# A rule that holds back side steps: when DeltaNet and attention matmuls enter the stream of weight matmuls in a hybrid decoder layer

## The chip, the cores and the metric

The kernel runs on one core of one Trainium2 chip. The metric is the device time of one execution in microseconds (us), the median of several runs. The core's engines work side by side, each through its own instructions in order: TensorE (PE: matmuls and transposes), VectorE (DVE), ScalarE (ACT), GpSimd (POOL) and SyncE (SP, which issues the DMAs). An instruction that waits for an operand holds up everything behind it on its engine.

## The reference

One decoder layer for 256 positions of width 1024 in fp32: a pre-norm, a joint input projection, two parallel branches, a gated merge, an output projection and a SwiGLU feed-forward block.

```
h = rms_norm(x, norm_mix_pre)
proj = h @ w_in                       # 1024 -> 9232: qa ka va qd kd vd zd bd ad ga gd
ya = moba_attention(rope(qa), rope(ka), va)      # 8 heads of 128, here one causal block of 256
yd = gated_deltanet(qd, kd, vd, zd, bd, ad, ...) # conv, silu, l2 norm, chunks of 64, 8 heads
merged = sigmoid(ga) * (ya @ w_o_attn) + sigmoid(gd) * (yd @ w_o_delta)
x = x + rms_norm(merged @ w_out, norm_mix_post)
h = rms_norm(x, norm_ffn_pre)
x = x + rms_norm((silu(h @ w_gate) * (h @ w_up)) @ w_down, norm_ffn_post)
# in the DeltaNet, per head and chunk: A = I + strict(beta k k^T * decay); T = A^-1 (unit lower triangular);
# u, w = T v_beta, T k_beta; then the state runs over the chunks; o = rms_norm(o) * silu(z)
```

## The kernel before

**Weight stream.** Most of PE's time goes into the weight matmuls, called main here. A weight matrix is cut into pieces of 128 x 1024 (824 or 828 in the gate columns). A piece is loaded into `wr` (4 buffers), ACT rounds it to `wh` (the high half), DVE subtracts to get `wl` (the low half), and three matmuls (high x high, high x low, low x high) make an fp32-accurate product. `wh` and `wl` have 5 buffers each, so that the `wh` of piece j waits until PE has done with piece j-5. `split_to` issues both operations three pieces ahead of their use. Main runs through the list `UNITS`: `c` (DeltaNet q, k, v by channel), `a` (attention q, k, v), `z`, `g` (gates), then `oa` and `od` (the branches' output projections), `wo`, and the feed-forward block. `oa` starts only when both attention generators are done, `od` when both of the DeltaNet's outputs are.

**Side steps.** The small matmuls of the branches (transposes through `tr`, L294; products through `mm`, L290) are made by generators: `dn` (a DeltaNet tile: group g of four heads, half t of the positions), `dno` (the DeltaNet's recurrence and output, per group), `at` (attention of four heads at a time) and `gates`. A DeltaNet tile computes k normalised (`d_kn`), its transpose `d_kh`, the matrix `h_a`, and inverts it in six levels with `h_U`, `h_T` and the level matrices `wl2` to `wl64` (traced as `wl`, 128x64 matmuls in fp16, four per step). At its end `dno` forms the output `d_oA`: ACT squares and sums four heads into `tiny` through `scr`, DVE, POOL (a power) and DVE again make a scale, four DVE operations SCALAR_TENSOR_TENSOR multiply by scale and `d_sz` (the silu of z), and PE transposes `d_oA` into `q_ydh` and `q_ydl`. A generator stops at `yield At(tiles)` until a built-in estimate of the engines' clocks says that the tiles are there (plus `MARGIN`, 50 ns), or for so many ns.

**What sets the order.** Class `Flow` keeps the estimated PE time `t`. Every main matmul group yields, and `run` then calls `pump`, which lets every generator whose time has come do its step, oldest first. Whatever a step issues on PE is put behind the main matmul that was last. The order on all engines is thus fixed when the program is built, by estimates; on the chip nothing is rearranged. In the trace a main matmul writes a bank `b_m`, a side matmul a bank `b_s`. A visit is a run of side matmuls between two main ones. Every operation of ACT, DVE, POOL and SP has the line L132, of the wrapper that accounts for it.

Of the kernel before, what the change touches and what calls it, by code (L numbers as in the profile page):

```python
# [26 lines left out]
NFR = DFF // 512  # L27
PSUM = bass.MemoryType.PSUM
MARGIN = 50
STAG = 0  # L30
WARM = 5
DEC = 6
# [105 lines left out]
class Flow:  # L138
# [65 lines left out]
    def step(self, s):  # L204
# [10 lines left out]
        if isinstance(w, At):  # L215
            del s[4:]
            s[0] = max(self.rdy.get(n, 0.0) for n in w.names) + MARGIN
        elif callable(w):
# [6 lines left out]
    def ready(self, s):  # L225
        return s[0] <= self.t and (len(s) == 4 or s[4]())

    def pump(self):
        for s in sorted(self.side, key=lambda a: a[1]):
            if self.ready(s):  # L230
                self.step(s)
# [21 lines left out]
def build(nc, tc, ctx, A):  # L253
# [756 lines left out]
    def unit_c(u):  # L1010
# [13 lines left out]
        if dns[g] == 6:  # L1024
            fl.add(("dn", g, 0), dn_tile(g, 0))
            fl.add(("dn", g, 1), later(STAG, dn_tile(g, 1)))
            fl.add(("dno", g), after(("dn", g, 0), dn_out, g))
# [327 lines left out]
    def later(ns, gen):  # L1355
        yield ns
        yield from gen

    def after(name, f, *args):
        while name not in fl.done:  # L1360
            yield 500
        yield from f(*args)
# [27 lines left out]
```

## Time and profile before

| | before |
|---|---|
| median of 3 runs | 549.88 us (549.68 to 550.12) |
| profiled execution | 549.29 us, span 547.6 us |
| PE busy | 534.8 us (98%) |
| DVE busy | 368.1 us (67%) |
| ACT busy | 315.0 us (58%) |
| POOL busy | 26.4 us (5%) |

The span runs from the first to the last profiled instruction; the remaining 1.69 us of the profiled execution lie around it. Busy shares say how full an engine is, not whether somebody waits for it: a DVE that is 67% busy can still be late for one matmul.

### The profile page before, as it was taken

What the parts mean: (1) busy time and instruction counts of PE and PEld (TensorE: products, weight loads), DVE (VectorE), ACT (ScalarE), POOL (GpSimd) and SP (SyncE); (2) the same over time, 40 slices, a digit from 0 to 9 for tenths busy, and PEclk for the clock granted to TensorE, in tenths of its full rate; (3) what the DMA queues carried; (4) which work ended last, traced back from release to release, by engine and by line L of the source; (5) the groups of instructions that cost most, each with busy time, mean ns of one, the idle gap of its engine ahead of it and who ended that gap; (6) DMA issues with size and microseconds to landing.
All of it is one profiled execution on the core that took longest, in us unless ns stands there. A gap on an engine that the chain in (4) does not pass through costs nothing.

```text
span 547.6 us, 8378 instructions
## 1 busy us (share of the span) xinstructions
PE 534.8 (98%) x3156; PEld 460.6 (84%) x3156; DVE 368.1 (67%) x650; ACT 315.0 (58%) x553; POOL 26.4 (5%) x38
## 2 busy tenths in 40 slices
PE   7999999899999999999999999999999999999995
PEld 5988898898989888899889988778888888888884
DVE  4899876895879787866577567586465554554434
ACT  6868658487654965786526544585444544443331
POOL 0000002200000230000000000010000000000000
PEclk8999999999999999999999999999999999999998
DMA  8947765245455252244465766257666665555612
GB/s 258 255 149 216 218 197 150 78 117 167 129 168 158 78 167 64 63 148 155 131 201 187 247 210 195 77 158 259 202 189 193 180 197 176 181 189 192 193 38 78
DMA packets 63035, 90.40 MB, mean 165 GB/s; under 512 B 3233, under 2 KB 35090, under 8 KB 62994
## 3 DMA queue, kind: packets, MB, share of 16 engines
q1 hardware_dynamic: 62994, 89.86, 53.4%
q8 instruction: 25, 0.41, 0.3%
q14 instruction: 16, 0.13, 0.1%
HBM read 88.80 MB, written 1.05 MB: 164 GB/s over the span
## 4 chain that ended last, share of the span: by engine, by line
PE 85%; DVE 4%; ACT 3%; DMA 3%; issue 2%; POOL 2%; SPq 0%; POOLq 0%; DVEq 0%; ACTq 0%
PE b_m L290 73%; PE b_s L290 8%; PE b_s L294 2%; PE b_m L294 2%; DMA q_x<-in_x 1%; DVE wl L132 1%; POOL tiny L132 1%; DMA K<-in_shape_k 1%; DMA wr<-in_w_in 1%; ACT wh L132 1%; ACT L132 0%; DVE h_a L132 0%; DVE q_vT L132 0%; SPq L132 0%; ACT d_js L132 0%
## 5 line engine op out<-in xcount | busy, mean ns | idle before, releaser
L132 DVE TENSOR_TENSOR wl<-wr,wh 128x1024 fp32r<-128x1024 f32 (+3 forms) x168 | 197.8, 1184 | 120.8 <-ACT wh L132 116.9
L132 ACT ACTIVATE wh<-wr 128x1024 fp32r<-128x1024 f32 (+3 forms) x168 | 171.8, 1030 | 151.6 <-PE b_m L290 142.9
L290 PE MATMUL b_m<-wh,q_fh 128*128 128x512 f32 x264 | 103.5, 392 | 0.5 <-DVE q_fl L132 0.5
L290 PE MATMUL b_m<-wl,q_fh 128*128 128x512 f32 x264 | 103.0, 390 | 0.0
L290 PE MATMUL b_m<-wh,q_fl 128*128 128x512 f32 x264 | 102.7, 390 | 0.0
L290 PE MATMUL b_m<-wh,q_hh 128*128 128x512 f32 (+2 forms) x208 | 83.1, 400 | 1.0 <-ACT wh L132 1.0
L290 PE MATMUL b_m<-wl,q_hh 128*128 128x512 f32 (+2 forms) x208 | 78.8, 379 | 0.0
L290 PE MATMUL b_m<-wh,q_hl 128*128 128x512 f32 (+2 forms) x208 | 78.8, 379 | 0.0
L290 PEld LDWEIGHTS b_m<-wh,q_fh 128*128 128x128 f32 x264 | 49.6, 188 | 11.0 <-DVE q_fl L132 1.0
L290 PEld LDWEIGHTS b_m<-wl,q_fh 128*128 128x128 f32 x264 | 49.6, 188 | 10.7 <-DVE wl L132 0.7
L290 PEld LDWEIGHTS b_m<-wh,q_fl 128*128 128x128 f32 x264 | 49.5, 188 | 10.3
L290 PE MATMUL b_m<-q_hh,wh 128*128 128x256 f32 x192 | 56.3, 293 | 0.0
L290 PE MATMUL b_m<-q_hl,wh 128*128 128x256 f32 x192 | 54.4, 283 | 0.0
L290 PE MATMUL b_m<-q_hh,wl 128*128 128x256 f32 x192 | 54.4, 283 | 0.0
L290 PEld LDWEIGHTS b_m<-wh,q_hh 128*128 128x128 f32 x208 | 39.5, 190 | 5.4 <-ACT wh L132 1.5
L290 PEld LDWEIGHTS b_m<-wh,q_hl 128*128 128x128 f32 x208 | 39.5, 190 | 5.3
L290 PEld LDWEIGHTS b_m<-wl,q_hh 128*128 128x128 f32 x208 | 39.6, 190 | 4.3 <-DVE wl L132 0.5
L132 POOL TENSOR_TENSOR tiny<-tiny,mhalf 128x4 f32<-128x4 f32 (+1 forms) x20 | 17.4, 873 | 471.3 <-DVE tiny L132 471.3
L290 PEld LDWEIGHTS b_m<-q_hh,wh 128*128 128x128 f32 x192 | 36.7, 191 | 0.4
L290 PEld LDWEIGHTS b_m<-q_hl,wh 128*128 128x128 f32 x192 | 36.7, 191 | 0.3
L290 PEld LDWEIGHTS b_m<-q_hh,wl 128*128 128x128 f32 x192 | 36.7, 191 | 0.1
L132 ACT ACTIVATE h_U<-b_s 128x256 f16<-128x256 f32 (+1 forms) x28 | 11.5, 415 | 10.9 <-PE b_s L290 10.9
(204 smaller groups left out, 718.0 us busy)
## 6 DMA issues: line engine op xcount, KB each, us to landing
wr<-in_w_in SPq DMA_DIRECT2D x56, 512.0 KB, 3.8
wr<-in_w_down SPq DMA_DIRECT2D x22, 512.0 KB, 3.3
wr<-in_w_gate SPq DMA_DIRECT2D x20, 512.0 KB, 3.7
wr<-in_w_up SPq DMA_DIRECT2D x20, 512.0 KB, 3.7
wr<-in_w_in SPq DMA_DIRECT2D x12, 412.0 KB, 3.4
wr<-in_w_o_attn SPq DMA_DIRECT2D x8, 512.0 KB, 4.4
wr<-in_w_o_delta SPq DMA_DIRECT2D x8, 512.0 KB, 4.2
wr<-in_w_out SPq DMA_DIRECT2D x8, 512.0 KB, 3.7
```

The lines of the kernel that those rows point to most:

```text
L132: r = f(*args, **kw)
L290: issue(lambda: PE.matmul(out, l, r, start=start, stop=stop))
L294: issue(lambda: PE.transpose(out, in_, idn))
```

## The change

A step that is ready is no longer always taken at once. `held` looks at the generators whose time has come. If one of them belongs to the DeltaNet or the gates (all but `at`), the whole visit is put off while another such generator is due within 700 ns and none has waited 700 ns. If only attention steps are ready, they are put off for up to 2500 ns as long as a DeltaNet generator exists. A put-off visit is tried again after the next main matmul group, and then all that is ready goes together. The computation is the same: 2383 main and 634 side matmuls in both kernels.

```diff
 MARGIN = 50
+HOLD = 700
+HOLD_AT = 2500
...
+    def held(self):
+        loose, tight, soon = [], [], False
+        for s in self.side:
+            if self.ready(s):
+                (loose if s[2][0] == "at" else tight).append(self.t - s[0])
+            elif len(s) == 4 and s[2][0] != "at" and s[0] <= self.t + HOLD:
+                soon = True
+        if tight:
+            return soon and max(tight) < HOLD
+        return bool(loose) and max(loose) < HOLD_AT and any(s[2][0] in ("dn", "dno") for s in self.side)
+
     def pump(self):
+        if self.held():
+            return
         for s in sorted(self.side, key=lambda a: a[1]):
             if self.ready(s):
                 self.step(s)
```

In the order of the built programs two stretches change: main matmuls 519 to 750 (head group 0, before at 95 to 149 us), with 25 visits before and 20 now, and 981 to 1307 (group 1, before at 210 to 300 us), with 36 and 43. Elsewhere the visits stand as they were. New lines stand 2 or 15 lower: L305 is the old L290, L309 the old L294, L134 the old L132.

**PE at the first transposes of group 0's k.** In PE's order before, `q_aq` is the attention's q of the same heads and `d_kn` the normalised k of both tiles:

```order
L290 MATMUL b_m<-q_hh_124,wl_1032 128x256
L294 MATMUL b_s<-ident,q_aq_610 128x128 x4
L290 MATMUL b_m<-q_hh_126,wh_1031 128x256
...
L290 MATMUL b_m<-q_hh_126,wl_1032 128x256
L294 MATMUL b_s<-ident,d_kn 128x128 x8
L294 MATMUL b_s<-ident,q_aq_610 128x128 x4
```

And the same place in the changed kernel:

```order
L305 MATMUL b_m<-q_hh_124,wl_1032 128x256
L305 MATMUL b_m<-q_hh_126,wh_1031 128x256
L305 MATMUL b_m<-q_hl_127,wh_1031 128x256
...
L305 MATMUL b_m<-q_hh_126,wl_1032 128x256
L309 MATMUL b_s<-ident,d_kn 128x128 x8
L309 MATMUL b_s<-ident,q_aq_610 128x128 x4
```

The four `q_aq` transposes that stood before the `d_kn` visit now stand behind it (and the second four behind the next visit).

**ACT at the silu of z of group 1.** ACT's order before, with `d8_p0` and `q15_p1` the attention's exponentials, `d13_sz01` and `d7_sz11` the two halves of `d_sz`, `q11_ydh0` the evacuation of the first transposed `d_oA`, `h8_U` and the like the copies that the level steps wait for:

```order
L132 ACTIVATE d8_p0_2767,tiny_96<-b4_s_2769,tiny_96 128x128 x4
L132 ACTIVATE scr_97,tiny_96<-d1_oA_2356 128x128 x4
L132 ACTIVATE q15_p1_2768,tiny_96<-b1_s_2818,tiny_96 128x256 x2
L132 ACTIVATE q15_p1_2768,tiny_96<-b7_s_2835,tiny_96 128x256 x2
L132 ACTIVATE wh63_2910<-wr63_2594 128x828
L132 ACT_TABLE_LOAD
L132 ACTIVATE d13_sz01_2904<-b3_m_2588,tiny_96 128x512
L132 ACTIVATE q11_ydh0_2320<-b0_s_2876,colp_95 128x4x128
L132 ACTIVATE h8_U_2540<-b4_s_2883 128x16x16
L132 ACTIVATE h2_T_2480<-b2_s_2889 128x16x16
L132 ACTIVATE h4_U_2559<-b5_s_2895 128x16x16
L132 ACTIVATE d7_sz11_2906<-b6_m_2589,tiny_96 128x512
```

And in the changed kernel, where the two halves are `d12_sz01` and `d7_sz11`:

```order
L134 ACTIVATE scr_97,tiny_96<-d1_oA_2356 128x128 x4
L134 ACTIVATE d8_p0_2804,tiny_96<-b7_s_2806,tiny_96 128x128 x4
L134 ACTIVATE wh63_2898<-wr63_2594 128x828
L134 ACTIVATE q11_ydh0_2320<-b5_s_2861,colp_95 128x4x128
L134 ACTIVATE q15_p1_2805,tiny_96<-b3_s_2827,tiny_96 128x256 x2
L134 ACT_TABLE_LOAD
L134 ACTIVATE d12_sz01_2892<-b4_m_2588,tiny_96 128x512
L134 ACT_TABLE_LOAD
L134 ACTIVATE q15_p1_2805,tiny_96<-b6_s_2844,tiny_96 128x256 x2
L134 ACTIVATE h8_U_2540<-b2_s_2883 128x16x16
L134 ACT_TABLE_LOAD
L134 ACTIVATE d7_sz11_2894<-b0_m_2589,tiny_96 128x512
```

An exponential now stands between the two silus, so that the table is loaded three times here and not once; over the whole program it is 14 loads, and 12 before.

**DVE and ACT at the last DeltaNet output.** DVE's order before, from the last addition to `d_oA` to its four scalings:

```order
L132 TENSOR_TENSOR d6_oA_3348<-b6_s_3491,d6_oA_3348 128x512
L132 TENSOR_TENSOR wl82_3535<-wr82_3425,wh82_3534 128x824
L132 SCALAR_TENSOR_TENSOR tiny_96<-tiny_96 128x4
L132 TENSOR_SCALAR tiny_96<-tiny_96 128x4
L132 TENSOR_TENSOR tiny_96<-tiny_96 128x4
L132 SCALAR_TENSOR_TENSOR d6_oA_3348<-d6_oA_3348,tiny_96,d7_sz11_2906 128x128 x4
```

The same on DVE in the changed kernel:

```order
L134 TENSOR_TENSOR d6_oA_3375<-b7_s_3521,d6_oA_3375 128x512
L134 TENSOR_TENSOR wl84_3575<-wr84_3465,wh84_3574 128x1024
L134 TENSOR_TENSOR wl85_3600<-wr85_3492,wh85_3599 128x1024
L134 SCALAR_TENSOR_TENSOR tiny_96<-tiny_96 128x4
L134 TENSOR_SCALAR tiny_96<-tiny_96 128x4
L134 TENSOR_TENSOR tiny_96<-tiny_96 128x4
L134 SCALAR_TENSOR_TENSOR d6_oA_3375<-d6_oA_3375,tiny_96,d7_sz11_2894 128x128 x4
```

And on ACT in the changed kernel, where before the four `scr` stood in one run with no other work between them:

```order
L134 ACTIVATE scr_97,tiny_96<-d6_oA_3375 128x128
L134 ACTIVATE q17_gt82081_3183<-b4_m_3435,tiny_96 128x412
L134 ACTIVATE scr_97,tiny_96<-d6_oA_3375 128x128
L134 ACTIVATE wh84_3574<-wr84_3465 128x1024
L134 ACTIVATE scr_97,tiny_96<-d6_oA_3375 128x128
L134 ACTIVATE wh85_3599<-wr85_3492 128x1024
L134 ACTIVATE scr_97,tiny_96<-d6_oA_3375 128x128
```

Two weight pieces of 1024 columns now stand in the chain from `d_oA` to its scaling, where one of 824 stood. On PE, 39 main matmuls stand between the `d_at` products and the first transpose of `d_oA`, and 33 before; the four transposes are taken as 1, 1 and 2, with a main matmul after each of the first two. The last matmul that reads piece 80, whose buffer piece 85 takes, is 18 main matmuls ahead of the first transpose.

## Rows read from the trace of the kernel before

**Rows 1.** The page's head: span, busy time and instructions of each engine.

```profile
span 547.6 us, 8378 instructions
PE 534.8 (98%) x3156; PEld 460.6 (84%) x3156; DVE 368.1 (67%) x650; ACT 315.0 (58%) x553; POOL 26.4 (5%) x38
```

**Rows 2.** Windows: span, busy PE, PEld, DVE, ACT, POOL, granted clock, DMA share, GB/s.

```profile
205.00:262.00 57.00, 57.00 (x446) 49.75 (x446) 41.22 (x86) 39.09 (x85) 2.29 (x3) 1.00 0.36 111
```

**Rows 3.** Timeline, all engines, 95 to 99 us: start, duration, work, idle before.

```profile
95.45 0.60 PE L294 MATMUL b_s<-ident,q_aq 128*128 128x128 f32 x4
95.81 0.36 PE L290 MATMUL b_m<-q_hh,wh 128*128 128x256 f32 x1
...
96.60 0.60 PE L294 MATMUL b_s<-ident,d_kn 128*128 128x128 f32 x4
96.64 1.01 POOL L132 TENSOR_TENSOR tiny<-tiny,mhalf 128x4 f32<-128x4 f32 x1 [2.02 <-DVE tiny L132]
...
97.68 0.69 DVE L132 TENSOR_TENSOR d_kn<-b_s,tiny 128x512 f32<-128x512 f32 x1 [1.12 <-POOL tiny L132]
98.29 1.22 DVE L132 TENSOR_TENSOR wl<-wr,wh 128x1024 fp32r<-128x1024 f32 x1
...
98.52 0.63 PE L294 MATMUL b_s<-ident,d_kn 128*128 128x128 f32 x4 [1.31 <-DVE d_kn L132]
```

**Rows 4.** Timeline of PE, main matmuls behind an fp16 visit and behind a scores visit.

```profile
111.77 0.36 PE L290 MATMUL b_m<-q_hh,wh 128*128 128x256 f32 x1
111.97 0.28 PE L290 MATMUL b_m<-q_hl,wh 128*128 128x256 f32 x1
112.09 0.28 PE L290 MATMUL b_m<-q_hh,wl 128*128 128x256 f32 x1
...
115.07 0.47 PE L290 MATMUL b_m<-q_hh,wh 128*128 128x256 f32 x1
115.38 0.28 PE L290 MATMUL b_m<-q_hl,wh 128*128 128x256 f32 x1
```

**Rows 5.** Timeline of PE at a level step late in group 0.

```profile
142.68 0.28 PE L290 MATMUL b_m<-q_hh,wl 128*128 128x256 f32 x1
142.99 0.28 PE L290 MATMUL b_s<-h_U,h_a 128*128 128x64 f16 x4
```

**Rows 6.** Timeline, all engines, first output of group 1: from `d_at` to the scaling.

```profile
223.46 1.05 PE L290 MATMUL b_s<-d_vn,d_at 128*128 128x128 f32 x8
...
227.81 0.16 DVE L132 SCALAR_TENSOR_TENSOR tiny<-tiny 128x4 f32<-128x4 f32 x1
...
229.72 1.14 DVE L132 SCALAR_TENSOR_TENSOR d_oA<-d_oA,tiny,d_sz 128x128 f32<-128x128 f32 x4
```

**Rows 7.** Timeline of ACT at the table load for the silu of z.

```profile
230.77 0.89 ACT L132 ACTIVATE wh<-wr 128x828 fp32r<-128x828 f32 x1
231.68 1.28 ACT L132 ACT_TABLE_LOAD   x1
232.97 0.69 ACT L132 ACTIVATE d_sz<-b_m,tiny 128x512 f32<-128x512 f32 x1
```

**Rows 8.** Timeline, all engines, last output: from `d_at` to the transposes of `d_oA`.

```profile
291.85 1.05 PE L290 MATMUL b_s<-d_vn,d_at 128*128 128x128 f32 x8
292.65 0.44 PE L290 MATMUL b_m<-wh,q_hh 128*128 128x412 f32 x1
...
294.29 0.29 ACT L132 ACTIVATE scr<-d_oA 128x128 f32<-128x128 f32 x1
...
296.02 0.16 DVE L132 SCALAR_TENSOR_TENSOR tiny<-tiny 128x4 f32<-128x4 f32 x1 [0.58 <-ACT scr L132]
...
297.70 1.14 DVE L132 SCALAR_TENSOR_TENSOR d_oA<-d_oA,tiny,d_sz 128x128 f32<-128x128 f32 x4
...
298.54 1.05 ACT L132 ACTIVATE wh<-wr 128x1024 fp32r<-128x1024 f32 x1
...
298.95 0.60 PE L294 MATMUL b_s<-ident,d_oA 128*128 128x128 f32 x4
```

## The prediction

> **What bounds the kernel now.** I read the page's head first: PE is busy 534.8 of 547.6 us, 98% [rows 1]. Then the windows by stage: from 205 to 262 us PE is busy 57.00 of 57.00 us at a granted clock of 1.00 [rows 2]. So PE sets the time, and a change of order that adds no matmul can move the end only by (a) what PE loses at the switch from a side visit back to main, and (b) time in which PE stands at a side matmul whose operand is late. I then went through PE's timeline for both.
>
> For (b) the largest place is the transposes of `d_kn` in group 0: tile A starts at 96.60, tile B only at 98.52, where four transposes 0.11 apart would have started at 97.0. PE lost 1.5 us, of which the row shows 1.31 as idle. The chain behind it runs POOL's power at 96.64 (1.01 us), then DVE's `d_kn` from 97.68 to 98.37 [rows 3]. A second place is 142.99, where `h_U` starts 0.31 after the last main matmul instead of 0.12 to 0.14: 0.17 us [rows 5].
>
> For (a): behind an fp16 visit the second main matmul starts 0.20 us after the first (111.77, 111.97), the third 0.12 later (112.09), so a visit with an fp16 end costs 0.08 to 0.09. Behind 256-column scores it is 0.31 (115.07, 115.38), so 0.18 to 0.19 [rows 4]. Behind transposes I find 0.01, behind 128-column fp32 products 0.03; the counts of these hardly enter.
>
> **The change part by part.** No operation goes or comes but two table loads on ACT; all else is order.
>
> *Visits.* Group 0, by what a visit ends with, before: 12 fp16 level steps x 0.09, one other fp16 step 0.08, 2 scores x 0.18, 3 fp32 products x 0.03, 7 transposes x 0.01 = 1.68 us. After: 8 x 0.09 + 2 x 0.18 + 3 x 0.03 + 7 x 0.01 = 1.24. So **-0.44**. Group 1, before: 5 level steps and 9 other fp16 steps, 11 fp32, 9 transposes, 2 scores = 0.45 + 0.72 + 0.33 + 0.09 + 0.36 = 1.95; after 12, 7, 10, 12 and 2 of them = 1.08 + 0.56 + 0.30 + 0.12 + 0.36 = 2.42. So **+0.47**: the rule merges visits in group 0 and multiplies them in group 1, where the steps of tile and recurrence no longer fall together. Price bounds of 0.08 and 0.09 change the pair's sum by under 0.05.
>
> *The wait for d_kn.* Before, the four `q_aq` transposes (95.45 to 95.81, with the slower main matmul behind them 0.44 us of PE's time) stand ahead of the `d_kn` visit [rows 3]; after, they stand behind it. POOL and DVE keep their order there, so `d_kn` B comes at 98.37 as before while PE is there 0.44 earlier: **+0.44**. The transposes are not lost work, so the gain of doing them later is nothing: PE waits where it worked.
>
> *The wait at 142.99.* After, 12 main matmuls stand ahead of that step and not 6, 0.7 us more of cover: **-0.17** [rows 5].
>
> *First output of group 1.* In before PE has 18 main matmuls of 512 columns between the visit at 223.46 and the transposes of `d_oA` at 231.21 and doesn't wait. The chain takes 227.81 - 223.46 = 4.35 us to the scale and 229.72 - 223.46 = 6.26 to the first scaling, done 7.4 after the visit's start for the last head [rows 6]. After, side visits fill most of the gap: counting matmuls at these durations PE is there 7.1 us after the `d_at` products. Before, four exponentials stood ahead of the `scr`; now four copies of level steps do, which are as short in sum (the scaling begins about 6.7 and ends at 7.8). PE's four transposes wait for one head each; I take **+0.4**, with 0 (the scr run without a gap) and 0.6 as bounds.
>
> *Table loads.* One load takes 1.28 us, and the operation behind it starts 0.01 later: 231.68 + 1.28 to 232.97 [rows 7]. Between the `scr` of the first output and the `h_U` copy that PE waits for two level steps on, ACT's queue now holds four loads (the last ahead of the gates), three exponential runs, two silus and four `wh`: 16.9 us by distances from start to start (a `wh` of 828 columns 0.91, a load 1.29, a silu 0.59 [rows 7]; the others from their own rows in the same way), 18.05 by whole durations. PE gets there after 16.1 + 0.4 us, and ACT starts about 0.9 ahead. So the copy comes 0.5 us early by the one and 0.65 late by the other. Distances are what a queue shows, so I take **0**; bounds 0 and 0.7. What covers the loads is main matmuls alone; without that cover each costs PE 1.28. [...]
>
> *Last output.* Before, PE starts the `d_at` products at 291.85 and the transposes of `d_oA` at 298.95, 7.10 us later; the last scaling ends at 298.84, so the chain was 0.11 us ahead of PE [rows 8]. There is no slack to give. The 33 main matmuls between take (298.95 - 292.65 - 0.09) / 33 = 0.188 us each. After, there are 39, so PE comes to the first transpose 6 x 0.188 = 1.13 us later, at t + 8.23, t being the start of the products. But DVE now has two `wl` of 1024 columns ahead of the scale (1.22 us each [rows 3]) in place of one of 824, and the second, `wl85`, needs `wh85`, which on ACT stands behind two gates, `wh84` (1.05 [rows 8]) and three `scr`, and needs the buffer of piece 80. PE is done with piece 80 only 18 main matmuls ahead of the transposes, 18 x 0.188 = 3.4 us. From there: 0.1 to 0.2 to be told, 1.05 for `wh85`, 1.22 for `wl85`, then from the scale to the last scaling 297.70 + 1.14 - 296.02 = 2.82. Sum 5.2 to 5.3 against 3.4 and the 0.6 us that PE's three other transposes and two main matmuls take: late by 1.2 to 1.3. By ACT's queue alone (first `scr` at t + 2.44 as in 294.29, then 4.0 us of gates, `scr`, `wh84` and `wh85`, and 1.22 + 2.82) the last head is there at t + 10.5 to 10.6 where PE wants it at t + 8.8: late by 1.7. I take **+1.5**. Bounds: 0 if ACT runs early enough that `wh85` isn't behind the gates and the buffer is told sooner, 2.0 if both add.
>
> *What else could wait.* `oa` and `od` start later in main than these places, with over 20 matmuls of group 0's output between; I find nothing else late. DMA issue order is unchanged: main's pieces come in the same sequence, and only side steps move past it.
>
> **Sum.** -0.44 + 0.47 + 0.44 - 0.17 + 0.4 + 0 + 1.5 = +2.2 us. Against the profiled execution's own 549.29 (547.6 of span and 1.69 around it) that is 551.5; the median of the runs shown lies 0.59 above that execution, so 549.88 + 2.2 = **552.1 us**.
>
> **Rivals.**
> *A, faster.* Operands may be ready earlier than rows of another order say. If `d_kn` B is ready at 97.0 and not at 98.37, its wait goes (-1.5), no new wait comes, and -0.44 + 0.47 - 0.17 - 1.5 = -1.6: 548.2. It decides at 1.4 us of lead for POOL's power. For it: POOL idles 2.02 us ahead of the power [rows 3], so what feeds it could come sooner. Against it: POOL and DVE have the same order there in both kernels.
> *B, no change.* The two new waits at `d_oA` don't come, because ACT starts its `scr` and `wh` earlier than I place them; then -0.44 + 0.47 + 0.44 - 0.17 = +0.3: 550.2. For it: both estimates rest on a chain put together from rows of another order. Against it: the buffer of piece 80 is PE's own doing and doesn't move.
> *C, slower still.* ACT's queue with the loads counts by durations: PE waits 0.7 us more at the level step: 552.8, or 553.3 with the upper bound at the first output and more of the last.
> [...]
>
> **How the numbers follow.** The forecast 0.48, B 0.27, C 0.14, A 0.08, D 0.03. Slower holds the forecast, C and D, 0.65; within 0.2% (1.1 us either way, about what a measurement of this kernel can tell from no change) B, 0.27; faster A, 0.08. The range reaches down to B less some of its spread, 549.9, and up to 554.0, which takes in C and 2.0 at the last output; it leaves out A, D and the lower part of B, under 0.2. The forecast's own range, by its bounds, is 551.0 to 553.5.
>
> **What would show it.** In the profile of the changed kernel: PE's idle at `d_kn` B is about 1.75 where it was 1.31; no `h_U` gap late in group 0; `q_aq` transposes behind `d_kn`; two more table loads on ACT, with the next operation right behind each; PE waits for DVE at both `d_oA` transposes of group 1, the last one for over 1 us, with `wl85` of 1.22 us just ahead of DVE's scale. I am wrong if PE's busy share in 262 to 302 us stays at 100%, if the level step behind the loads waits over 1 us, or if `d_kn` comes earlier.

## The result

The changed kernel takes 553.32 us (552.58 to 553.36, 4 runs) against 549.78 us (549.25 to 550.12, 4 runs) before: 3.5 us more, a ratio of 1.0061 with a 95% interval of 1.0049 to 1.0074. The forecast was 552.1 in a range of 549.9 to 554.0, slower at 0.65.

The page's head of the changed kernel, to be held against [rows 1]:

```profile
span 551.6 us, 8373 instructions
PE 536.6 (97%) x3156; PEld 459.9 (83%) x3156; DVE 368.1 (67%) x650; ACT 315.9 (57%) x555; POOL 26.5 (5%) x38
```

PE has the same 3156 matmuls, of which 2384 write a bank `b_m` and 772 a bank `b_s` in both traces (these counts, and not 2383 and 634, are the ones to go by), and is busy for 97% of a longer span. ACT has two operations more, the table loads. The windows of the changed kernel (columns as in [rows 2]):

```profile
205.00:262.00 57.00, 56.77 (x440) 48.87 (x439) 38.65 (x81) 40.96 (x87) 2.77 (x4) 1.00 0.36 114
262.00:300.00 38.00, 38.00 (x222) 33.33 (x221) 26.44 (x48) 15.13 (x25) 1.02 (x1) 1.00 0.56 177
300.00:310.00 10.00, 8.93 (x50) 8.44 (x49) 6.11 (x12) 6.60 (x15) 1.01 (x1) 1.00 0.54 163
```

PE now idles 0.23 us in a stretch in which it idled not at all before, and 1.07 us between 300 and 310. The granted clock is 1.00 in all of these, so it isn't the clock. From 262 to 302 us PE is busy for 40.00 of 40.00 us: the wait at the last output falls behind that stretch, as shown below.

Busy shares don't say where 4.0 us of span went. For that I take the start of the same main matmul in both traces (main is numbered through, 0 to 2383) and subtract. The table has this for all kernels of this study; each column is a difference of two starts, or of the last start and the span's end, in us.

| kernel | to no. 100 | 518 to 760 (group 0) | 970 to 1323 (group 1) | 1323 to 2383 | 2383 to the end | median |
|---|---|---|---|---|---|---|
| before | 23.81 | 56.30 | 100.40 | 233.90 | 6.55 | 549.78 |
| after | 24.65 | 56.45 | 102.89 | 233.58 | 7.51 | 553.32 |
| hold_only | 24.38 | 56.43 | 102.89 | 233.65 | 7.65 | 553.34 |
| at_only | 24.40 | 56.33 | 100.39 | 233.84 | 6.55 | 550.01 |
| g0_only | 24.37 | 56.45 | 100.39 | 233.63 | 6.55 | 549.75 |
| g1_only | 24.38 | 56.31 | 102.89 | 233.63 | 6.55 | 551.93 |
| after_pin | 24.24 | 56.45 | 101.59 | 233.59 | 6.85 | 551.28 |
| after_table | 25.15 | 56.43 | 102.73 | 233.63 | 7.63 | 553.46 |
| rtpin | 24.98 | 56.09 | 100.40 | 233.83 | 6.56 | 550.27 |
| g0rt | 23.83 | 56.21 | 100.39 | 233.60 | 6.55 | 549.44 |
| padA | 24.34 | 56.43 | 102.89 | 233.50 | 7.64 | 553.30 |
| padV | 24.96 | 56.45 | 102.91 | 233.54 | 6.54 | 552.03 |
| g0kn | 24.50 | 55.27 | 100.40 | 233.56 | 6.55 | 548.41 |
| knpin | 24.55 | 54.73 | 100.39 | 233.90 | 6.55 | 548.70 |

The stretches left out (100 to 518 and 760 to 970) differ by 0.3 and 0.04 us at most over all kernels. In the two middle columns a stretch with the same order agrees to 0.03 us in every kernel, so they tell far more than a median, whose runs spread over 1 us. The first column is the exception: it lies anywhere from 23.81 to 25.15 in kernels whose first instructions are the same. A load at the start takes longer in one profile than in the other: the 512 KB of `q_x`, issued at 3.05 in both, land 6.79 us later before and 7.75 in the changed kernel.

From before to after: group 0 +0.15, group 1 +2.49, the rest of the stream -0.32, the end +0.96, and 0.84 of start that is scatter.

Nearly all of the -0.32 lies at one place. ScalarE's square `d_js`, ahead of the feed-forward part, starts 0.34 us behind the end of its wait for PE in the four kernels without the rule (before, at_only, rtpin, knpin: 347.54 to 347.88 in before) and 0.06 behind it in the ten with any of it (350.94 to 351.00 in after), and the transposes of `q_xr` on PE move with it. The order is the same in all; why ScalarE starts later in the four stays open.

**Group 0.** The changed kernel's timeline at `d_kn`, as in [rows 3]:

```profile
96.05 1.22 DVE L134 TENSOR_TENSOR wl<-wr,wh 128x1024 fp32r<-128x1024 f32 x1
...
97.18 0.16 DVE L134 TENSOR_SCALAR tiny<-tiny 128x4 f32<-128x4 f32 x1
...
97.42 1.01 POOL L134 TENSOR_TENSOR tiny<-tiny,mhalf 128x4 f32<-128x4 f32 x1 [2.01 <-DVE tiny L134]
...
98.47 0.69 DVE L134 TENSOR_TENSOR d_kn<-b_s,tiny 128x512 f32<-128x512 f32 x1 [1.12 <-POOL tiny L134]
...
99.30 0.63 PE L309 MATMUL b_s<-ident,d_kn 128*128 128x128 f32 x4 [1.75 <-DVE d_kn L134]
```

The idle time is 1.75 where it was 1.31 (tile A's transposes start at 96.95, so that tile B's could start at 97.39 and not at 99.30: 1.91 late, and 1.47 before by the same count): the chain of `wl`, the small TENSOR_SCALAR behind it, POOL's power and `d_kn` runs as before, and PE is there 0.44 earlier because the `q_aq` transposes now stand behind.

**Group 1, last output.** Timeline of the changed kernel, to be held against [rows 8]:

```profile
297.40 1.05 PE L305 MATMUL b_s<-d_vn,d_at 128*128 128x128 f32 x8
...
302.27 2.50 DVE L134 TENSOR_TENSOR wl<-wr,wh 128x1024 fp32r<-128x1024 f32 x2 [2.64 <-ACT wh L134]
...
302.44 1.06 ACT L134 ACTIVATE wh<-wr 128x1024 fp32r<-128x1024 f32 x1
303.41 0.29 ACT L134 ACTIVATE scr<-d_oA 128x128 f32<-128x128 f32 x1
...
304.68 0.15 DVE L134 SCALAR_TENSOR_TENSOR tiny<-tiny 128x4 f32<-128x4 f32 x1
...
305.12 1.01 POOL L134 TENSOR_TENSOR tiny<-tiny,mhalf 128x4 f32<-128x4 f32 x1 [27.54 <-DVE tiny L134]
...
306.36 1.14 DVE L134 SCALAR_TENSOR_TENSOR d_oA<-d_oA,tiny,d_sz 128x128 f32<-128x128 f32 x4
306.86 0.30 PE L309 MATMUL b_s<-ident,d_oA 128*128 128x128 f32 x1 [1.07 <-DVE d_oA L134]
```

Two `wl` of 1.2 us stand ahead of the scale at 304.68, which had its last `scr` at 303.8. The `d_at` products began at 297.40, so the scale is at t + 7.28, where the prediction's way through the buffer of piece 80 comes to t + 7.2 to 7.3, and the first transpose at t + 9.46 and not at the t + 8.23 of the order alone: 1.23 us of wait, of which the row shows 1.07 as idle. `wh85` is the row at 302.44. PE's last matmul on piece 80 ends at 302.40 by the trace, and ACT's queue has no idle time ahead of `wh85` either, so the buffer and the queue let it go at the same moment; which of the two set it can't be told.

**Group 1, the level step behind the table loads.** Timeline of ACT and PE of the changed kernel, as in [rows 7]:

```profile
233.76 1.28 ACT L134 ACT_TABLE_LOAD   x1
...
235.06 0.69 ACT L134 ACTIVATE d_sz<-b_m,tiny 128x512 f32<-128x512 f32 x1
...
235.75 1.28 ACT L134 ACT_TABLE_LOAD   x1
237.05 0.48 ACT L134 ACTIVATE q_p<-b_s,tiny 128x256 f32<-128x256 f32 x1
...
237.54 0.34 PE L305 MATMUL b_m<-wl,q_hh 128*128 128x414 f32 x1
...
237.96 0.38 ACT L134 ACTIVATE h_U<-b_s 128x256 f16<-128x256 f32 x1
...
238.12 0.28 PE L305 MATMUL b_s<-wl,h_T 128*128 128x64 f16 x4 [0.23 <-ACT q_p L134]
```

Each load takes 1.28 us and the next operation starts 0.02 or less behind it. A level step waits behind these two; it starts 0.58 us behind the main matmul before it where 0.19 is usual, so it is 0.39 late.

**The end.** DMA of the changed kernel in its last 4 us (share of the 16 engines in 40 equal slices, then packets, then by queue):

```profile
DMA  0899998999999620001000000000000000000000
...
DMA packets 289, 0.53 MB, mean 121 GB/s; under 512 B 32, under 2 KB 32, under 8 KB 288
...
q14 instruction: 1, 0.01, 0.5%
```

Among the packets of the last output store, which is issued at 547.54, stands one of the queue that loads instructions: 8192 bytes, from 549.20 to 549.54. Three packets of the store start only as it ends (549.53 to 549.86). Before, the last such load is at 540.95, 3.5 us ahead of the last store's issue, and every packet of that store has started 1.68 us behind the issue; here the last one starts 2.31 behind it. SyncE waits 1.0 us longer for this store to land (us in total, times, longest; first before, then the changed kernel):

```profile
SPq L1377 <- DMA out<-d_yw: 1.7, 1, 1.7
...
SPq L1392 <- DMA out<-d_yw: 2.7, 1, 2.7
```

Whether the three packets waited for the load isn't shown: the trace doesn't name the DMA engine of a packet. The packets end 0.66 us later and the wait 0.96; where the other 0.3 go stays open.

### The profile page after: what moved, and what is told of

It reads as the page before. It is cut to its first block, busy times and chain, and to the rows that moved or that the text cites. A ratio compares the mean times of both kernels' runs of the same rounds, so it can differ in the third digit from the quotient of the medians.

```text
span 551.6 us, 8373 instructions
## 1 busy us (share of the span) xinstructions
PE 536.6 (97%) x3156; PEld 459.9 (83%) x3156; DVE 368.1 (67%) x650; ACT 315.9 (57%) x555; POOL 26.5 (5%) x38
## 3 DMA queue, kind: packets, MB, share of 16 engines
HBM read 88.80 MB, written 1.05 MB: 163 GB/s over the span
## 4 chain that ended last, share of the span: by engine, by line
PE 83%; ACT 5%; DVE 4%; issue 2%; DMA 2%; POOL 2%; SPq 0%; POOLq 0%; DVEq 0%; ACTq 0%
PE b_m L305 72%; PE b_s L305 8%; PE b_s L309 2%; PE b_m L309 2%; DMA q_x<-in_x 1%; POOL tiny L134 1%; ACT L134 1%; DVE wl L134 1%; ACT wh L134 1%; ACT scr L134 1%; DMA wr<-in_w_in 1%; DVE tiny L134 1%; DVE h_a L134 0%; DVE q_vT L134 0%; SPq L134 0%
## 5 line engine op out<-in xcount | busy, mean ns | idle before, releaser
L134 DVE TENSOR_TENSOR wl<-wr,wh 128x1024 fp32r<-128x1024 f32 (+3 forms) x168 | 197.9, 1185 | 116.8 <-ACT wh L134 116.2
L134 ACT ACTIVATE wh<-wr 128x1024 fp32r<-128x1024 f32 (+3 forms) x168 | 171.9, 1032 | 153.0 <-PE b_m L305 142.3
L305 PE MATMUL b_m<-wh,q_fh 128*128 128x512 f32 x264 | 103.5, 392 | 0.5 <-DVE q_fl L134 0.5
L305 PE MATMUL b_m<-wl,q_fh 128*128 128x512 f32 x264 | 103.0, 390 | 0.0
L305 PE MATMUL b_m<-wh,q_fl 128*128 128x512 f32 x264 | 102.7, 390 | 0.0
L305 PE MATMUL b_m<-wh,q_hh 128*128 128x512 f32 (+2 forms) x208 | 83.5, 402 | 1.5 <-ACT wh L134 1.5
L305 PE MATMUL b_m<-wh,q_hl 128*128 128x512 f32 (+2 forms) x208 | 79.0, 380 | 0.0
L305 PE MATMUL b_m<-wl,q_hh 128*128 128x512 f32 (+2 forms) x208 | 78.7, 379 | 0.0
L305 PEld LDWEIGHTS b_m<-wh,q_fh 128*128 128x128 f32 x264 | 49.6, 188 | 11.0 <-DVE q_fl L134 1.0
L305 PEld LDWEIGHTS b_m<-wl,q_fh 128*128 128x128 f32 x264 | 49.6, 188 | 10.6 <-DVE wl L134 0.7
L305 PEld LDWEIGHTS b_m<-wh,q_fl 128*128 128x128 f32 x264 | 49.6, 188 | 10.4
L305 PE MATMUL b_m<-q_hh,wh 128*128 128x256 f32 x192 | 55.8, 290 | 0.0
L305 PE MATMUL b_m<-q_hl,wh 128*128 128x256 f32 x192 | 54.4, 284 | 0.0
L305 PE MATMUL b_m<-q_hh,wl 128*128 128x256 f32 x192 | 54.3, 283 | 0.0
L305 PEld LDWEIGHTS b_m<-wh,q_hh 128*128 128x128 f32 x208 | 39.6, 190 | 6.4 <-ACT wh L134 2.4
L305 PEld LDWEIGHTS b_m<-wh,q_hl 128*128 128x128 f32 x208 | 39.4, 189 | 5.3
L305 PEld LDWEIGHTS b_m<-wl,q_hh 128*128 128x128 f32 x208 | 39.5, 190 | 4.1 <-DVE wl L134 0.3
L134 POOL TENSOR_TENSOR tiny<-tiny,mhalf 128x4 f32<-128x4 f32 (+1 forms) x20 | 17.4, 875 | 474.5 <-DVE tiny L134 474.5
L305 PEld LDWEIGHTS b_m<-q_hh,wh 128*128 128x128 f32 x192 | 36.7, 191 | 0.3
L305 PEld LDWEIGHTS b_m<-q_hl,wh 128*128 128x128 f32 x192 | 36.7, 191 | 0.3
L305 PEld LDWEIGHTS b_m<-q_hh,wl 128*128 128x128 f32 x192 | 36.7, 191 | 0.0
```

The costliest lines, as they stand in the source:

```text
L134: r = f(*args, **kw)
L305: issue(lambda: PE.matmul(out, l, r, start=start, stop=stop))
```

## The experiments

The first column of the table names each run. Each changes one thing, in the changed kernel, in the kernel before, or in one of the runs.

**hold_only**: `HOLD_AT = 0`.

```diff
-HOLD_AT = 2500
+HOLD_AT = 0
```

> The attention rule is switched off (HOLD_AT = 0), the 700 ns rule stays. The order of every engine comes out the same as in the changed kernel, so this is the changed kernel a second time, with a second profile. Of the 4.0 us by which the changed kernel's span is longer, 2.3 lie between the first weight matmuls and the last one, 0.8 in the first 10 us (the first weight piece landed later) and 0.9 behind the last matmul (the last output store). My theory: the 0.8 and the 0.9 are scatter of the loads and stores, and the order is worth 2.3 us. Then this run is at 552.0 to 553.5 and the first weight matmul starts anywhere between 8.0 and 9.0 us. Rival: the changed kernel's start and end are slower in every run. Then the start is again near 9.0, the end again 7.5 us behind the last matmul, and the time again 553.3.

553.34 us (ratio to before 1.0063, 1.0051 to 1.0076). The start came at 24.38, between the two others; the end again at 7.65. So the theory held for the start and fell for the end: the longer end belongs to the kernel. And the attention rule of 2500 ns does nothing: with it and without it the order is the same on every engine.

**at_only**: `HOLD = 0`.

```diff
-HOLD = 700
+HOLD = 0
```

> The 700 ns rule is switched off (HOLD = 0), the attention rule of 2500 ns stays. The order of every engine comes out the same as before the change, so this is the kernel before a second time. Expected within 0.4 us of before, 549.4 to 550.2. Its profile shows how far the start (first weight matmul at 8.03 before) and the end (6.6 us behind the last matmul before) move by themselves: if they are scatter, by up to 1 us each; by the rival they stay within 0.2 us.

550.01 us (1.0006, 0.9995 to 1.0017). Start 0.59 later than in the profile of before, end the same 6.55. The start is scatter.

**g0_only** and **g1_only**: the rule in one head group alone.

```diff
     def pump(self):
-        if self.held():
+        if not any(s[2] in (("dn", 1, 0), ("dn", 1, 1), ("dno", 1), ("at", 1)) for s in self.side) and self.held():
             return
```

(and without the `not` for the other.)

> The rule holds only until the first generator of head group 1 is there, so that group 0 has the new order and group 1 the old one. Theory (prediction's terms: visits -0.44, the wait for d_kn +0.44, the wait late in group 0 -0.17; the two traces give +0.15 for this stretch): between -0.3 and +0.3 us against before, 549.5 to 550.1. Rival: the five visits fewer are worth their 0.44 and more by themselves: -0.6 or below.

> The rule holds only once a generator of head group 1 is there, so that group 0 has the old order and group 1 the new one. Theory: this stretch carries the loss, +2.2 to +2.6 us against before (the traces show +2.5 in it), 552.0 to 552.4, and g0_only and this add up to the whole. Rival: the parts need each other (a later arrival out of group 0 makes the waits of group 1): under +1.5 here.

g0_only 549.75 us (0.9995, 0.9986 to 1.0003), g1_only 551.93 us (1.0036, 1.0023 to 1.0049). By stretch the parts add up exactly: g0_only has after's 56.45 in group 0 and before's 100.39 in group 1, g1_only the other way round. The loss in the stream is group 1's, and it needs nothing from group 0. The medians don't add up (-0.2 and +2.0 against +3.4): neither half has the longer end of the whole (1.0), and each of the two has the gain of 0.27 from 1323 on, which the whole has only once; some 0.3 is left for scatter.

**after_pin**: the last output's chain in one piece again, in the changed kernel.

```diff
+            if (t, g) == (1, 1):
+                fl.pin = [last_scr.ins, last_scaling.ins]
...
-            ACT.activation(hi, r, AF.Copy)
-            DVE.tensor_tensor(lo, r, hi.bitcast(F32), op=ALU.subtract)
+            if fl.pin:
+                with tc.issue_after(fl.pin[0]):
+                    ACT.activation(hi, r, AF.Copy)
+                with tc.issue_after(fl.pin[1]):
+                    DVE.tensor_tensor(lo, r, hi.bitcast(F32), op=ALU.subtract)
```

> The changed kernel, with one thing mended: the splits of weight pieces from 83 on are put behind the last output's chain, wh behind its last scr on ACT and wl behind its last scaling on DVE, so that the chain runs in one piece as before. Theory: PE's wait at the last transposes of d_oA goes (1.23 us at the first and some 0.4 behind it), so -1.6 us against the changed kernel, 551.5 to 552.0. Rival: the pieces put back are late for main, which waits instead by up to 1 us: -0.6 or less; or the wait was ACT's and DVE's queue as a whole and only moves: 0.

551.28 us (1.0028, 1.0016 to 1.0039). DVE and PE of this kernel:

```profile
301.50 0.16 DVE L134 SCALAR_TENSOR_TENSOR tiny<-tiny 128x4 f32<-128x4 f32 x1 [2.57 <-ACT scr L134]
...
303.19 1.14 DVE L134 SCALAR_TENSOR_TENSOR d_oA<-d_oA,tiny,d_sz 128x128 f32<-128x128 f32 x4
...
304.25 0.60 PE L310 MATMUL b_s<-ident,d_oA 128*128 128x128 f32 x4
```

No wait is left at the transposes (the first is at t + 7.10, as before), and group 1 is 1.30 us shorter, not 1.6: the 0.4 that was expected at the three other transposes isn't there. The edit moves more than the splits: the built-in estimates follow, and PE takes the four transposes in one visit, 33 main matmuls behind the products and not 39. So the 1.30 is the price of the chain together with the split visit. The rivals fall: main doesn't wait for the pieces put back. The other 0.7 of the median, which takes it below the 551.5 to 552.0 expected, lies in the end (6.85 against 7.51 to 7.65) and in scatter.

**after_table**: both silus of z behind the last exponential, 12 table loads instead of 14.

```diff
-            ACT.activation(z, v4(outs[t]), AF.Silu, scale=rs[t])
+            if n == 1:
+                with tc.issue_after(fl.ex):      # the last exponential so far
+                    ACT.activation(z, v4(outs[t]), AF.Silu, scale=rs[t])
+            else:
+                ACT.activation(z, v4(outs[t]), AF.Silu, scale=rs[t])
```

> The changed kernel, with the two silus of z of group 1 put behind the last exponential, so that 12 table loads are left of 14 and the level step's copies no longer stand behind three of them. Theory: PE's wait of 0.39 us at the level step (238.12 in the changed kernel) goes and the rest stays, -0.4 us, 552.8 to 553.0; some order moves with it, worth 0.1 either way. Rival: the two loads cost their 2.6 us: 550.7.

553.46 us (1.0067, 1.0055 to 1.008), over the 552.8 to 553.0 expected. The wait at the level step is gone, but group 1 is only 0.16 us shorter: the same exchange splits two visits more (45 and not 43), and the rest of the 0.39 went there. The loads cost what they hold up, not their 2.6 us.

**rtpin** and **g0rt**: two instructions of DVE exchanged at `d_kn`, in the kernel before and in g0_only.

```diff
+        if (g, t) == (0, 1):
+            fl.rt = small_tensor_scalar.ins
...
-            DVE.tensor_tensor(lo, r, hi.bitcast(F32), op=ALU.subtract)
+            if j == 31:
+                with tc.issue_after(fl.rt):
+                    DVE.tensor_tensor(lo, r, hi.bitcast(F32), op=ALU.subtract)
```

(and for all other pieces as before.)

> The kernel before, with two instructions of DVE exchanged: the small TENSOR_SCALAR that feeds POOL's power for d_kn of the second tile goes ahead of the 1.22 us wl of piece 31. Nothing else moves on any engine. Theory: POOL's power starts at 95.5 and not at 96.64, d_kn B is there at 97.2 and not 98.37, and PE's wait of 1.47 us shrinks to 0.3: -1.1 us against before, 548.7. Rival: the wl behind it is late for main, or PE waits for something else that came just ahead of d_kn: within 0.3 of before.

> The rule in group 0 only, and the two instructions of DVE exchanged as in the kernel of the same exchange. Theory: the transposes of q_aq that the rule moved behind d_kn leave PE at d_kn 0.44 us earlier, so that 0.75 of the wait of 1.91 is left; -1.1 against the rule in group 0 only, and -1.0 to -1.3 against before, 548.5 to 548.8. Rival: with the wait gone the fewer visits of group 0 show for the first time: -1.6 or below, 548.2.

rtpin 550.27 us (1.0002, 0.9993 to 1.0011), g0rt 549.44 us (0.9989, 0.998 to 0.9998). Group 0 got 0.21 to 0.24 us shorter, not 1.1. The theories fell, and the rival of g0rt with them; rtpin's rival holds by its number (within 0.3 of before) but not by either cause it names. DVE and POOL of rtpin show why:

```profile
96.54 0.16 DVE L132 TENSOR_SCALAR tiny<-tiny 128x4 f32<-128x4 f32 x1
96.60 1.22 DVE L132 TENSOR_TENSOR wl<-wr,wh 128x1024 fp32r<-128x1024 f32 x1
...
98.72 0.69 DVE L132 TENSOR_TENSOR d_kn<-b_s,tiny 128x512 f32<-128x512 f32 x1 [0.90 <-POOL tiny L132]
```

```profile
96.77 1.91 POOL L132 TENSOR_TENSOR tiny<-tiny,mhalf 128x4 f32<-128x4 f32 x1 [0.88 <-DVE tiny L132]
```

POOL's power came 1.1 us earlier against the stream, and then took 1.91 us where every one shown so far took 1.01.

**g0kn** and **knpin**: the same `wl` put behind `d_kn` instead, so that DVE is idle while POOL works; in g0_only and in the kernel before. The edit is that of rtpin with `d_kn` of the second tile in place of the TENSOR_SCALAR.

> The rule in group 0 only, and wl of piece 31 put behind d_kn of the second tile on VectorE; nothing else moves. In the two kernels with the exchange that put it between the small TENSOR_SCALAR and d_kn, POOL's power took 1.91 us with that wl beside it and 1.01 without, so that d_kn came no more than 0.2 us earlier. Theory: the wl held POOL. With VectorE idle the power takes 1.01, d_kn B is there 2.0 us behind d_kn A's start and not 3.0, and PE's wait at d_kn falls from 1.91 to 0.8: -1.1 against the rule in group 0 only (549.75), 548.6. Rival: POOL's power is long for another reason (its own start, or a fetch), 1.91 again and no gain: 549.7.

g0kn 548.41 us (0.9979, 0.997 to 0.9988). POOL and DVE:

```profile
96.43 1.01 POOL L134 TENSOR_TENSOR tiny<-tiny,mhalf 128x4 f32<-128x4 f32 x1 [0.88 <-DVE tiny L134]
```

```profile
95.58 0.69 DVE L134 TENSOR_TENSOR d_kn<-b_s,tiny 128x512 f32<-128x512 f32 x1 [1.12 <-POOL tiny L134]
96.19 0.16 DVE L134 TENSOR_SCALAR tiny<-tiny 128x4 f32<-128x4 f32 x1
97.47 0.69 DVE L134 TENSOR_TENSOR d_kn<-b_s,tiny 128x512 f32<-128x512 f32 x1 [1.12 <-POOL tiny L134]
```

With DVE idle the power takes 1.01, and `d_kn` of the second tile starts 1.89 us behind the first instead of 3.03 in the changed kernel (95.44 to 98.47). Group 0 is 1.18 us shorter than in g0_only. It was the `wl` beside it that held POOL.

> The kernel before, without the rule, and wl of piece 31 put behind d_kn of the second tile on VectorE as in the run with the rule in group 0 only; nothing else moves. It tells whether the rule is worth anything once that wait is mended. Theory: PE's wait at d_kn of 1.47 falls to about 0.3, -1.2 us against before, 548.5, the same as with the rule in group 0 (548.41) within what can be told, since the transposes of q_aq fill part of the wait here and the fewer visits save about as much there. Rival: the rule's five visits fewer now show in full: this run 0.3 to 0.5 us above the one with the rule in group 0, in the stretch from main matmul 518 to 760, 55.6 to 55.8 us against 55.27.

knpin 548.70 us (0.998, 0.9969 to 0.9991). Without the rule group 0 is shorter still, 54.73 against 55.27: PE's wait at `d_kn` is 0.34 here and 0.77 there, and the wait of 0.42 at `id,h_T`, which g0kn keeps, is gone too. Theory and rival both fell: with this wait mended, the rule in group 0 loses 0.5 us in this stretch. That g0kn's median isn't higher lies in part in the stretch from 1323 on, where the kernels with any of the rule take 233.50 to 233.65 and those without 233.83 to 233.90 (the 0.28 at ScalarE's `d_js`); the rest is scatter. Both beat before, by 1.0 to 1.3 us, and can't be told apart.

**padA** and **padV**: idle instructions in the changed kernel, to find whose instructions are loaded late.

```diff
+        for i in range(8):
+            ACT.activation(padt[:, i:i + 1], mhalf[:, 0:1], AF.Copy)
```

(padV: `range(4)` and `DVE.tensor_copy`.)

> The changed kernel with eight copies of one column more on ScalarE, in the feed-forward part, where it idles; nothing else moves on any engine. In the changed kernel, its repeat and the one with fewer table loads the end of the program lies 4.1 to 4.2 us behind the issue of the last output store, in all kernels with the old end 3.13 to 3.14; in the former the last load of instructions (8192 bytes on queue 14) starts at 549 us, behind the output, in the latter at 541 to 544, ahead of it. These kernels hold 766 to 768 records of ScalarE, the others 770 to 774. Theory: the last block of ScalarE's instructions is called for only when ScalarE comes near it, and with a few instructions fewer that is at the very end. With eight more the load comes at about 543, the end 3.13 us behind the last store, -1.0 us against the changed kernel: 552.3. Rival: it is VectorE's (833 or 834 records against 835 or 836), or chance: the end stays at 4.1 to 4.2 and the time at 553.3.

> The changed kernel with four copies of one column more on VectorE, at the same place; nothing else moves. VectorE then has 838 records, over the 835 and 836 of the kernels with the short end, and ScalarE still 767. Theory (ScalarE's instructions): the late load and the long end stay, 553.3. Rival (VectorE's): the end is 3.13 us behind the last store, 552.3.

padA 553.30 us (1.0066, 1.0053 to 1.0079), padV 552.03 us (1.0043, 1.0031 to 1.0055). The theory of ScalarE's instructions fell and the rival held: eight more on ScalarE change nothing (end 4.23 us behind the issue of the last store), four more on VectorE bring the last load forward to 544.3, 3.6 us ahead of that issue, and the end to 3.13. DMA of padV in its last 3.5 us, where no load of instructions is left:

```profile
DMA packets 288, 0.52 MB, mean 119 GB/s; under 512 B 32, under 2 KB 32, under 8 KB 288
...
q1 hardware_dynamic: 288, 0.52, 31.9%
```

## Why the prediction was right, point by point

**Direction and the main term held.** The last output was put at +1.5; the wait there is 1.23, and after_pin, which mends it, gives 1.30 back. Its way through the buffer of piece 80 gave 1.2 to 1.3 and was right link by link: 39 main matmuls instead of 33, `wl85` just ahead of the scale, `wh85` at t + 5.04, the scale at t + 7.28. The 0.1 to 0.2 to be told was an estimate (in [rows 3] PE starts 0.15 behind the end of `d_kn`, in [rows 8] 0.11 behind the last scaling's); `wh85` starts 0.04 behind PE's end at 302.40. Its other way, through ACT's queue, gave 1.7 and was too long: from the first `scr` (300.11) to the end of `wh85` (303.50) it took 3.4 us and not 4.0. That the buffer and not the queue set `wh85` isn't shown.

**The wait for d_kn** was +0.44 and measured 1.91 - 1.47 = +0.44. **The wait late in group 0** was -0.17 and went (0.19).

**The first output** was +0.4 and measured 0.15 (the fourth transpose starts 0.26 and not 0.11 behind the third), at the lower part of its bounds. **The table loads** were put at 0 with a bound of 0.7 and cost 0.39 of wait, but not where the prediction looked. It worked out the level step behind all four loads, and there PE waits 0.04 at most, as forecast; the 0.39 stands at the step behind the first two, for which it made no sum. D's chance of 0.03 stands for a load that holds ACT beyond its own 1.28 us, which no run shows: behind each of the four loads of the changed kernel from 233.76 to 246.56 ACT's next operation starts after 0.01 to 0.02 us.

**The visits** were the weakest term. In group 1, +2.49 less 1.30, 0.39 and 0.15 leaves 0.65 for them, where +0.47 stood. In group 0, 0.15 less 0.44 plus 0.19 leaves -0.10, where -0.44 stood: a merged visit changes from fp16 to fp32 inside itself, and pays there part of what it saves at its end. The starts of single matmuls in the two traces show part of it: the first transpose behind an fp16 matmul takes 0.145 us and not 0.11 (two such places in the changed kernel, none before), a 256-column score 0.30 and not 0.22 (three, two before), which makes 0.15 of the missing 0.34; the rest is read from the sum. The prices of 0.18 to 0.19 behind scores are too high, since the last score takes 0.03 of PE's time instead of 0.22; with two such visits in both kernels nothing hangs on it.

**What was missed** is 1.0 us behind the last matmul. The sum stood at +2.2 and the stream (group 0, group 1 and the rest, without start and end) came to 0.15 + 2.49 - 0.32 = +2.3; the end adds 1.0, and 3.3 is the 3.4 to 3.5 of the medians within their spread. The prediction looked at what the change does to the order and at no effect on the number of an engine's instructions. The -0.32 behind group 1 was not foreseen either; where it lies is shown above, its cause stays open.

**Luck.** That +2.2 and +2.3 lie so close is in part luck. Against the terms, the visits cost 0.34 and 0.18 more, the table loads 0.39 more, the last output 0.20 less, the first 0.25 less, and the 0.32 behind group 1 was won without a forecast: these nearly cancel. The time of 553.32 lies on rival C's 553.3 by chance, since C has its extra in the loads' queue and the first output, and the measured one is behind the last matmul.

**Two slips.** The lower bounds of the terms (0 at both outputs) come to 550.2, not to the 551.0 given as the forecast's own range. And between 223.46 and the transposes at 231.21 stand 21 main matmuls, not 18; no sum uses that count.

**The signs.** PE's idle at `d_kn` is 1.75, the late `h_U` gap is gone, the loads and `wl85` stand as described. One sign of being wrong came true by its letter: PE's busy share from 262 to 302 us is 100%. The window was set on the time scale of before. In the changed kernel the `d_at` products stand 18 main matmuls later, at 297.40 and not 291.85, and the wait at 305.8 to 306.9.

**The rivals.** A, that chains run earlier than the rows say, has nothing for it: the `d_kn` of the two tiles start 3.03 us apart, and 3.02 before. B fails at the last output. C's wait behind all four loads isn't there.

## What to carry to other kernels

Merging small steps into fewer visits earned a tenth of a microsecond a visit at best here (0.08 to 0.09 for a visit with an fp16 end by [rows 4]; the five visits fewer of group 0 left 0.10 in all); a step that comes later by a few matmuls can land its whole chain behind other work on VectorE and ScalarE and cost ten times that (the 1.30 that after_pin gives back), so look at what stands between the links of a chain, not at the number of visits. Where a short chain through GpSimd feeds TensorE, keep an operation of VectorE like `wl` out of it altogether: at `d_kn` a place between two links was nearly as bad as a place ahead of them (rtpin and g0rt made group 0 only 0.21 to 0.24 us shorter, g0kn with `wl` behind the chain 1.18). And measure by stretches between the same matmuls: the two middle columns agree to 0.03 us where the runs of one kernel spread over 1 us, and the columns show start, stream and end apart.

## What the hardware showed that was not expected

**GpSimd's power takes longer beside a `wl` of VectorE.** POOL's power on 128 x 4 takes 1.01 us by itself and 1.91 us when VectorE has begun a `wl` (1.22 us, `wl<-wr,wh`, which reads no bank) 0.17 us before it; in g0rt it is 1.91 again, with the same 0.17. The extra 0.90 is a little less than what was left of the `wl` (96.60 + 1.22 - 96.77 = 1.05). The kernel before already held such a case, in the feed-forward part, and so does the changed one (1.46 at 364.44):

```profile
361.14 1.22 DVE L132 TENSOR_TENSOR wl<-wr,wh 128x1024 fp32r<-128x1024 f32 x1
...
361.30 1.46 POOL L132 TENSOR_TENSOR tiny<-tiny,mhalf 128x1 f32<-128x1 f32 x1 [3.91 <-DVE tiny L132]
```

The power on 128 x 1 takes 0.55 to 0.56 everywhere else in this trace, also where VectorE has begun an operation of 0.68 to 0.69 us that reads a bank (`d_yw<-b_m,q_wmp`, 0.16 us before): so it is not any operation beside it that holds POOL. What in `wl` holds it the traces don't show.

**A few instructions fewer on VectorE made the end 1.0 us later.** In the nine kernels with 835 to 838 records of VectorE the last load of instructions comes at 540 to 544 us, 3.3 to 3.6 ahead of the issue of the last store, and the end 3.13 to 3.14 us behind that issue. In the four with 834 it comes at 549 to 550, 1.65 to 1.79 us behind the issue and among the store's packets, of which two or three start only as the load ends; the end is 4.10 to 4.24 behind the issue. The one with 833 (after_pin) shows that it is not the late load as such: there it comes at 549.76, behind the whole store, the wait for the store is 1.7 us as before, and the end, at 3.44, is 0.3 late, as is VectorE's last instruction but one, which comes at 3.08 and not at 2.72. Four idle instructions on VectorE undo the 1.0 (padV: load at 544.3, end at 3.13). Why the number of VectorE's instructions moves that load by 5 us the trace doesn't show.
